# Four buffers for split weight blocks, S5 input by half quarters, and two RG-LRU steps on GpSimd in the first layer

## The chip, the core and the metric

The kernel runs on one core of one Trainium2 chip. The metric is the device time of one execution in microseconds; before the change it is 1570.3 us (median of three runs, 1568.19 to 1570.87).

The core has five engines that run their own instruction queues in order and meet through semaphores. TensorE (PE) multiplies matrices, with its weight loads shown apart (PEld); VectorE (DVE), ScalarE (ACT) and GpSimd (POOL) work element by element; SyncE (SP) issues most of the DMAs, GpSimd the rest. Matrix products leave their sums in PSUM, everything else lives in SBUF, and SBUF holds what DMAs bring from HBM.

## The reference

Two layers over 512 latent and 256 context tokens of width 1024. Each layer norms and modulates its input, projects it with one matrix whose columns feed three branches (attention, RG-LRU, S5), multiplies each branch by its SiLU gate, projects it, merges the three by sigmoid gates, and adds the result back. The two recurrent branches, cut to what the change touches:

```python
def rglru_branch(...):
    u_l = depthwise_conv(x_l, conv_w, conv_b); u_c = depthwise_conv(x_c, conv_w, conv_b)
    for d, rev in enumerate((False, True)):
        a_c, b_c = rglru_coeffs(u_c, ...)        # a = exp(log_a), b = sqrt(1 - a^2) * (i * x)
        h_c = linear_scan(a_c, b_c, None, rev)   # h_t = a_t h_(t-1) + b_t
        h0 = h_c[:, 0] if rev else h_c[:, -1]
        a_l, b_l = rglru_coeffs(u_l, ...)
        hs_l.append(linear_scan(a_l, b_l, h0, rev)); hs_c.append(h_c)
    return hs_l[0] + hs_l[1], hs_c[0] + hs_c[1]

def s5_branch(u_l, u_c, ...):                     # per group of 16 channels, 64 complex states
    for d, rev in enumerate((False, True)):
        ar, ai, bbr, bbi = s5_discretise(...)
        cr_, ci_ = complex_scan(ar, ai, *drive(u_c, bbr, bbi), None, rev)
        lr_, li_ = complex_scan(ar, ai, *drive(u_l, bbr, bbi), (cr_[:, idx], ci_[:, idx]), rev)
        ...
    return readout(u_l, ...), readout(u_c, ...)
```

## The kernel before

Activations are kept transposed, 128 channels to a tile, with the 512 latent and 256 context tokens along the free axis (TT = 768 columns). All large products are made in three passes of float32r matmuls: both operands are split into a high and a low part, and `product` (L170) adds high x high, low x high and high x low, key tile by key tile. A weight block is 128 x 512 numbers (four key tiles of one 128-column output), and an input projection (`inproj`, L771) uses two of them.

`wsplit` (L154) makes a block ready. SyncE loads it into `wr` (L161), ScalarE copies it to the high part `wh` (L162), and the low part `wl` comes from VectorE as `wr - wh` (L167). In layer 0, from after the S5 input projection until `merge_y` of the S5 branch, `by_dma` is set: ScalarE writes `-wh` into `wl` (L164), and GpSimd issues a DMA that adds `wr` to it (L165). The pool `pW` keeps three tiles each of `wr`, `wh` and `wl`; some callers pass another pool or keep their tiles elsewhere.

The RG-LRU (`lru`, L810) runs four times per layer, for 128 channels at a time. It projects, convolves, makes four small products for the gates, and then: `th` gets a square root (L853), `gi` is multiplied by it (L854, 128x1536, both directions at once), two forward scans write `ys` (L855, L856), the reverse scan writes `hb` into `th` (L858), and `ys` and `hb` are added (L859, 128x768). L854 to L859 are VectorE's. Every working tile of this pool has one buffer, so the next RG-LRU waits for this one's.

S5 runs in 16 steps of two groups (`step`, L697). `s5_input` (L592) loads a quarter of the S5 input, 128 channels, into `vt` with eight DMAs from DRAM on SyncE; two buffers of 128x8x128 numbers. `s5_scan(pa)` (L600) multiplies it, turns it (`U`, `Wt`, L623 and L624, from PSUM), scans it (L629), turns it back and leaves the states in `st`; `s5_out(pa)` (L656) makes the outputs and reads `vt` again. The next quarter's input is asked for at the step before its first scan (L705).

RG-LRU calls, S5 steps and the gates' projections are mixed by a table (`PLAN`, L35): in layer 0 all 16 S5 steps lie beside the RG-LRU calls and the products that follow them. On every engine the order of the instructions is fixed when the kernel is built. It isn't the order of the source: a block's `wh` is made several products ahead, as far as the buffers reach.

Of the kernel before, what the change touches and what calls it, by code (L numbers as in the profile page):

```python
# [11 lines left out]
F32 = mybir.dt.float32  # L12
# [17 lines left out]
NCH = 96  # L30
NCC = 32
NCE = 128
# [19 lines left out]
def hybrid_kernel(ctx, tc, xT, cc, wmod, win, winv, wbr, wout, wglu, wlru, par, lqk, s5a, s5b, s5B, s5C, dsk, rope, outT):  # L52
# [101 lines left out]
    def wsplit(src, n, p=None, bufs=3, keep=None):  # L154
        p = p or pW
        raw = p.tile([128, 512], F32, name="wr", tag="wr", bufs=bufs)
        if keep:
            p, bufs = keep, None
        wh = p.tile([128, 512], F32R, name="wh", tag="wh", bufs=bufs)
        wl = p.tile([128, 512], F32R, name="wl", tag="wl", bufs=bufs)  # L160
        SP.dma_start(raw, src)  # L161
        S.activation(wh, raw, AF.Copy)  # L162
        if by_dma[0]:
            S.activation(wl, f32(wh), AF.Copy, scale=-1.0)  # L164
            G.dma_start(wl, raw, accum_op=OP.add)  # L165
        else:
            V.tensor_sub(wl, raw, f32(wh))  # L167
        return wh.rearrange("p (k n) -> p k n", n=n), wl.rearrange("p (k n) -> p k n", n=n)
# [385 lines left out]
    def s5_make(l):  # L554
# [34 lines left out]
                return (sps[pa][:, :R_WS].rearrange("p (q n) -> p q n", q=4),  # L589
                        tps[pa // 2][:, pa % 2 * 2:pa % 2 * 2 + 2])  # L590

        def s5_input(qt):  # L592

            vt = p5.tile([128, 8, NCE], F32, name="vt", tag="vt", bufs=2)
            for s in range(8):
                SP.dma_start(vt[s * 16:(s + 1) * 16],
                             usd[qt * 128:(qt + 1) * 128, s, :].rearrange("(g h) c -> h g c", h=16))
            vts[qt] = vt

        def s5_scan(pa):  # L600
            pr = pa % 4
            vt, (tb, ws) = vts[pa // 4], turn(pa)

            px = mis("ps_x")
            for d in range(2):
                for c in range(2):
                    for g in range(2):
                        v = vt[:, 2 * pr + g, :NCH] if d == 0 else vt[:, 2 * pr + g, NCE - 1:NCE - 1 - NCH:-1]
                        PE.matmul(px[64 * g:64 * g + 64, (c * 2 + d) * NCH:(c * 2 + d + 1) * NCH],  # L609
                                  lhsT=ws[:, 2 * d + g, 64 * c:64 * c + 64], rhs=v, start=True, stop=True)  # L610
            pxv = px[:, :4 * NCH].rearrange("p (c d j) -> p c d j", c=2, d=2)

            sh = [128, 2, 2, NCH]
            Cb = tb[:, 0].unsqueeze(1).to_broadcast(sh)
            Sb = tb[:, 1].unsqueeze(1).to_broadcast(sh)
            U = p5.tile([128, 2, 2, NCH], F32, name="U", tag="U")
            Wt = p5.tile([128, 2, 2, NCH], F32, name="W", tag="W")
            xx = p5.tile([128, 2, 2, NCH], F32, name="xx", tag="xx", bufs=2)
            for d in range(2 if need else 0):
                b = l * 32 + 2 * pa + d  # L620
                S.activation(dec[:, :, d, 1:], ones[:, 0:1].unsqueeze(2).to_broadcast([128, 2, NCH - 1]), AF.Copy,
                             scale=rho[:, b:b + 1])
            V.tensor_mul(U, pxv, Cb)  # L623
            V.tensor_mul(Wt, pxv, Sb)  # L624
            V.tensor_add(xx[:, 0], U[:, 0], Wt[:, 1])
            V.tensor_sub(xx[:, 1], U[:, 1], Wt[:, 0])
            if need:
                xf = xx.rearrange("p c d j -> p (c d j)")
                V.tensor_tensor_scan(xf, dec.rearrange("p c d j -> p (c d j)"), xf, 0.0, op0=OP.mult, op1=OP.add)  # L629
            else:  # L630
                for d in range(2):
                    b = l * 32 + 2 * pa + d
                    for c in range(2):
                        V.tensor_tensor_scan(xx[:, c, d], rho[:, b:b + 1].to_broadcast([128, NCH]), xx[:, c, d], 0.0,
                                             op0=OP.mult, op1=OP.add)
            U2 = p5.tile([128, 2, 2, NCH], F32, name="U2", tag="U")
            W2 = p5.tile([128, 2, 2, NCH], F32, name="W2", tag="W")
            js = slice(0 if need else NCC - 1, NCH - 1)
            V.tensor_mul(U2[..., js], xx[..., js], Cb[..., js])
            V.tensor_mul(W2[..., js], xx[..., js], Sb[..., js])  # L640
            st = sts[pa % 2]
            if not need:
                for g in range(2):
                    ps = slice(64 * g, 64 * g + 64)
                    V.tensor_sub(st[0:64, g, :, js.start + 1:NCH], U2[ps, 0, :, js], W2[ps, 1, :, js])
                    V.tensor_add(st[64:128, g, :, js.start + 1:NCH], U2[ps, 1, :, js], W2[ps, 0, :, js])
                return
            V.tensor_sub(xx[:, 0, :, js], U2[:, 0, :, js], W2[:, 1, :, js])
            V.tensor_add(xx[:, 1, :, js], U2[:, 1, :, js], W2[:, 0, :, js])

            for g in range(2):
                for c in range(2):
                    S.activation(st[64 * c:64 * c + 64, g, :, js.start + 1:NCH], xx[64 * g:64 * g + 64, c, :, js], AF.Copy)
            S.activation(st[:, :, 0, NCH:], st[:, :, 0, :NCC], AF.Copy)

        def s5_out(pa):  # L656

            pr = pa % 4
            vt, (vf, tp), st = vts[pa // 4], reach(pa), sts[pa % 2]
            py = mis("ps_y")  # L660
            for g in range(2):
                o = py[:, g * NCL:(g + 1) * NCL]
                PE.matmul(o, lhsT=tp[:, g, :], rhs=vt[:, 2 * pr + g, NCC:NCC + NCL], start=True,
                          stop=False)
                PE.matmul(o, lhsT=vf[:, g, 32:160], rhs=st[:, g, 0, NCC:NCC + NCL], start=False, stop=False)  # L665
                PE.matmul(o, lhsT=vf[:, 2 + g, 0:128],
                          rhs=st[:, g, 1, NCH - 1::-1] if need else st[:, g, 1, NCH - 1:NCC - 1:-1], start=False,
                          stop=True)
# [28 lines left out]
        def step(pa):  # L697
            if pa == 0:
                s5_input(0)
                s5_scan(0)  # L700
            if l == 0 and done[0] < 16:
                s5_inner(done[0])
                done[0] += 1
            if pa + 1 < 16:
                if pa % 4 == 3:  # L705
                    s5_input(pa // 4 + 1)
                    if l == 0:
                        whole(s5_tables(l, pa // 4 + 1, p5, pr_.tbs))
                s5_scan(pa + 1)
# [8 lines left out]
    for l in range(L):  # L718
# [91 lines left out]
        def lru(i):  # L810
# [40 lines left out]
            V.scalar_tensor_tensor(th, a2, 1.0, th, op0=OP.add, op1=OP.mult)  # L851
            V.scalar_tensor_tensor(gi, gi, 1.0, u.unsqueeze(1).to_broadcast([128, 2, TT]), op0=OP.add, op1=OP.mult)
            S.activation(th, th, AF.Sqrt, scale=0.25, bias=tiny[:, 0:1])  # L853
            V.tensor_mul(gi, gi, th)  # L854
            V.tensor_tensor_scan(ys[:, T:], r[:, 0, T:], gi[:, 0, T:], 0.0, op0=OP.mult, op1=OP.add)  # L855
            V.tensor_tensor_scan(ys[:, :T], r[:, 0, :T], gi[:, 0, :T], ys[:, TT - 1:TT], op0=OP.mult, op1=OP.add)  # L856
            hb = th[:, 0]
            V.tensor_tensor_scan(hb[:, ::-1], r[:, 1, ::-1], gi[:, 1, ::-1], 0.0, op0=OP.mult, op1=OP.add)  # L858
            V.tensor_add(ys[:, :W], ys[:, :W], hb[:, :W])  # L859
            return ys  # L860

        m_t = [pMm.tile([128, W], F32, name="m", tag="m") for _ in range(KT)]
# [482 lines left out]
```

## Time and profile before

| | us |
|---|---|
| median of three runs | 1570.3 (1568.19 to 1570.87) |
| the profiled execution, its own time | 1571.9 |
| its span, first to last instruction | 1570.1 |
| TensorE busy | 1489.2 (95%) |
| VectorE busy | 1125.0 (72%) |
| ScalarE busy | 818.7 (52%) |
| GpSimd busy | 172.2 (11%) |
| mean granted clock of TensorE | 0.98 of full speed |

The busy times say how much work each engine has, not where it waits: TensorE's 81 us of idle time are spread over stages whose limits differ. The profile is read stage by stage, with the windows first and then the waits and the time lines inside one stage.

### The profile page before, as it was taken

How to read it: one execution, taken by the hardware profiler on the slowest of the kernel's cores; microseconds unless marked ns; L12 is line 12 of the kernel's file. 1: busy time of each engine (PE TensorE's matmuls, PEld its weight loads, DVE VectorE, ACT ScalarE, POOL GpSimd, SP SyncE). 2: the span in 40 equal slices, each digit the busy share in tenths (PEclk: the TensorE clock that was granted, in tenths of full speed). 3: DMA queues.
4: the chain of work that ended last, by engine and by line, in shares of the span. 5: the costliest groups of instructions: out<-in, count | busy, mean ns of one | idle time of the engine just before them, and what ended most of it. 6: DMA issues, size and time to landing. Idle time of an engine off the chain costs nothing. (4 is left out here: it accounts for less than half of the span.)

```text
span 1570.1 us, 24750 instructions
## 1 busy us (share of the span) xinstructions
PE 1489.2 (95%) x9096; PEld 1246.2 (79%) x9096; DVE 1125.0 (72%) x2312; ACT 818.7 (52%) x1468; POOL 172.2 (11%) x231
## 2 busy tenths in 40 slices
PE   4998899899999999999999999999999999999997
PEld 2786778788988888888778887777788988888777
DVE  6789899978367757658568863789775488397555
ACT  6676878664344534534325365666525365355433
POOL 1111111124000100000332310000000000000110
PEclk8998999999999999989999999999999999999999
DMA  8555444467311111115573762435454212111542
GB/s 279 167 151 119 112 110 105 89 158 197 94 52 43 42 53 46 49 34 177 193 250 125 258 201 82 143 111 162 118 168 132 81 61 58 65 61 54 174 148 94
DMA packets 111210, 189.13 MB, mean 120 GB/s; under 512 B 25328, under 2 KB 42352, under 8 KB 111088
## 3 DMA queue, kind: packets, MB, share of 16 engines
q1 hardware_dynamic: 97392, 158.17, 32.2%
q0 software_dynamic: 13696, 29.37, 8.1%
q8 instruction: 72, 1.18, 0.3%
q14 instruction: 50, 0.41, 0.1%
HBM read 145.02 MB, written 25.69 MB: 109 GB/s over the span
## 5 line engine op out<-in xcount | busy, mean ns | idle before, releaser
L162 ACT ACTIVATE wh<-wr 128x512 fp32r<-128x512 f32 x320 | 200.3, 629 | 367.2 <-PE ps_in L180 151.3
L180 PE MATMUL ps_in<-hH,wh 128*128 128x512 f32 x1248 | 376.5, 360 | 14.4 <-ACT wh L162 7.3
L180 PE MATMUL ps_in<-hH,wl 128*128 128x512 f32 x1248 | 378.6, 359 | 7.1 <-DMA wl<-wr 7.1
L180 PE MATMUL ps_in<-hL,wh 128*128 128x512 f32 x1248 | 375.5, 359 | 0.0
L167 DVE TENSOR_TENSOR wl<-wr,wh 128x512 fp32r<-128x512 f32 x264 | 187.5, 714 | 172.7 <-ACT wh L162 129.9
L180 PEld LDWEIGHTS ps_in<-hH,wh 128*128 128x128 f32 x1248 | 207.3, 192 | 52.3 <-ACT wh L162 8.4
L180 PEld LDWEIGHTS ps_in<-hH,wl 128*128 128x128 f32 x1248 | 207.7, 191 | 43.1 <-DMA wl<-wr 9.6
L180 PEld LDWEIGHTS ps_in<-hL,wh 128*128 128x128 f32 x1248 | 206.9, 191 | 31.8
L911 POOL TENSOR_TENSOR m<-m,g 128x768 f32<-128x768 f32 (+1 forms) x16 | 29.0, 1811 | 730.7 <-issue 348.4
L1091 ACT ACTIVATE p<-ps_s,mx 128x768 f32<-128x768 f32 (+1 forms) x80 | 65.2, 815 | 71.4 <-DVE mx L1090 67.5
L180 PE MATMUL ps_b<-yH,wh 128*128 128x512 f32 (+1 forms) x288 | 89.5, 359 | 0.6 <-DVE m L945 0.6
L180 PE MATMUL ps_b<-yL,wh 128*128 128x512 f32 (+1 forms) x288 | 88.0, 357 | 0.0
L180 PE MATMUL ps_b<-yH,wl 128*128 128x512 f32 (+1 forms) x288 | 87.7, 357 | 0.0
L1089 DVE TENSOR_REDUCE mx<-ps_s 128x1 f32<-128x768 f32 (+1 forms) x80 | 67.6, 847 | 23.9 <-PE ps_s L1086 23.3
L165 POOL DMA_DIRECT2D wl<-wr x56 | 49.0, 896 | 259.6 <-ACT wl L164 206.1
L180 PEld LDWEIGHTS ps_b<-yH,wh 128*128 128x128 f32 x288 | 48.2, 188 | 10.7 <-ACT wl L164 0.9
L180 PEld LDWEIGHTS ps_b<-yL,wh 128*128 128x128 f32 x288 | 47.7, 188 | 7.2
L180 PEld LDWEIGHTS ps_b<-yH,wl 128*128 128x128 f32 x288 | 47.6, 188 | 7.2
L180 PE MATMUL acc<-mH,wh 128*128 128x512 f32 (+1 forms) x160 | 49.2, 340 | 0.0
L180 PE MATMUL acc<-mH,wl 128*128 128x512 f32 (+1 forms) x160 | 48.8, 337 | 0.0
L180 PE MATMUL acc<-mL,wh 128*128 128x512 f32 (+1 forms) x160 | 48.8, 337 | 0.0
L1107 DVE TENSOR_TENSOR wTL<-ps_t,wTH 128x512 fp32r<-128x512 f32 (+1 forms) x72 | 35.9, 536 | 13.4 <-ACT wTH L1106 13.2
(357 smaller groups left out, 2901.1 us busy)
## 6 DMA issues: line engine op xcount, KB each, us to landing
wr<-in_win SPq DMA_DIRECT2D x208, 256.0 KB
wm<-in_wmod SPq DMA_DIRECT2D x48, 512.0 KB
wl<-wr POOLq DMA_DIRECT2D x56, 256.0 KB, 3.9
wr<-in_wbr SPq DMA_DIRECT2D x48, 256.0 KB
sp<-s5d SPq DMA_DIRECT2D x16, 768.0 KB
wr<-in_wout SPq DMA_DIRECT2D x32, 256.0 KB
s5d<-vv POOLq DMA_DIRECT2D x16, 320.0 KB, 3.2
usd<-up SPq DMA_DIRECT2D x8, 512.0 KB
```

Of the source, the lines that this page charges most:

```text
L162: S.activation(wh, raw, AF.Copy)
L165: G.dma_start(wl, raw, accum_op=OP.add)
L167: V.tensor_sub(wl, raw, f32(wh))
L180: PE.matmul(out[:, c0:c0 + n], lhsT=(wl if ps == 2 else wh)[:, k, :], rhs=rhs(k0 + k, ps == 1)[:, t0:t0 + n], start=st, stop=en)
L911: (V if n == 0 and dt >= ADD_V[l] else G).tensor_add(m_t[dt][:, :W], m_t[dt][:, :W], g[:, :W])
L1089: V.reduce_max(mx[:, 0:1], sc[:, :kw], axis=AX.X)
L1091: S.activation(p[c][:, :kw], sc[:, :kw], AF.Exp, bias=mx[:, 1:2], scale=0.125, accum_out=sm[:, c:c + 1])
L1107: V.tensor_sub(wTL[:, k0:k1, qi * 128:(qi + 1) * 128], src, f32(wTH[:, k0:k1, qi * 128:(qi + 1) * 128]))
```

## The change

`wsplit` gives the high and low parts four buffers where they come from the pool `pW`; the raw tile keeps three. `s5_input` loads half a quarter (64 channels) into a tile of half the size, still with two buffers and eight DMAs each; it is asked for at every even step, for the half quarter that the step after it scans first. In `lru` of layer 0 the product L854 and the sum L859 go to GpSimd (`E = G`); layer 1 keeps them on VectorE. `vt` gives up 4 KB of each partition, and the two added weight tiles take 4 KB.

```diff
--- before.py
+++ after.py
@@ -156,6 +156,8 @@
         raw = p.tile([128, 512], F32, name="wr", tag="wr", bufs=bufs)
         if keep:
             p, bufs = keep, None
+        if p is pW:
+            bufs = 4
         wh = p.tile([128, 512], F32R, name="wh", tag="wh", bufs=bufs)
         wl = p.tile([128, 512], F32R, name="wl", tag="wl", bufs=bufs)
         SP.dma_start(raw, src)
@@ -589,23 +591,24 @@
                 return (sps[pa][:, :R_WS].rearrange("p (q n) -> p q n", q=4),
                         tps[pa // 2][:, pa % 2 * 2:pa % 2 * 2 + 2])
 
-        def s5_input(qt):
-
-            vt = p5.tile([128, 8, NCE], F32, name="vt", tag="vt", bufs=2)
+        def s5_input(hq):
+
+            vt = p5.tile([128, 4, NCE], F32, name="vt", tag="vt", bufs=2)
             for s in range(8):
                 SP.dma_start(vt[s * 16:(s + 1) * 16],
-                             usd[qt * 128:(qt + 1) * 128, s, :].rearrange("(g h) c -> h g c", h=16))
-            vts[qt] = vt
+                             usd[hq * 64:(hq + 1) * 64, s, :].rearrange("(g h) c -> h g c", h=16))
+            vts[hq] = vt
 
         def s5_scan(pa):
             pr = pa % 4
-            vt, (tb, ws) = vts[pa // 4], turn(pa)
+            vt, (tb, ws) = vts[pa // 2], turn(pa)
 
             px = mis("ps_x")
             for d in range(2):
                 for c in range(2):
                     for g in range(2):
-                        v = vt[:, 2 * pr + g, :NCH] if d == 0 else vt[:, 2 * pr + g, NCE - 1:NCE - 1 - NCH:-1]
+                        v = vt[:, 2 * (pr % 2) + g]
+                        v = v[:, :NCH] if d == 0 else v[:, NCE - 1:NCE - 1 - NCH:-1]
                         PE.matmul(px[64 * g:64 * g + 64, (c * 2 + d) * NCH:(c * 2 + d + 1) * NCH],
                                   lhsT=ws[:, 2 * d + g, 64 * c:64 * c + 64], rhs=v, start=True, stop=True)
             pxv = px[:, :4 * NCH].rearrange("p (c d j) -> p c d j", c=2, d=2)
@@ -656,11 +659,11 @@
         def s5_out(pa):
 
             pr = pa % 4
-            vt, (vf, tp), st = vts[pa // 4], reach(pa), sts[pa % 2]
+            vt, (vf, tp), st = vts[pa // 2], reach(pa), sts[pa % 2]
             py = mis("ps_y")
             for g in range(2):
                 o = py[:, g * NCL:(g + 1) * NCL]
-                PE.matmul(o, lhsT=tp[:, g, :], rhs=vt[:, 2 * pr + g, NCC:NCC + NCL], start=True,
+                PE.matmul(o, lhsT=tp[:, g, :], rhs=vt[:, 2 * (pr % 2) + g, NCC:NCC + NCL], start=True,
                           stop=False)
                 PE.matmul(o, lhsT=vf[:, g, 32:160], rhs=st[:, g, 0, NCC:NCC + NCL], start=False, stop=False)
                 PE.matmul(o, lhsT=vf[:, 2 + g, 0:128],
@@ -698,12 +701,13 @@
             if pa == 0:
                 s5_input(0)
                 s5_scan(0)
+            if pa % 2 == 0 and pa < 14:
+                s5_input(pa // 2 + 1)
             if l == 0 and done[0] < 16:
                 s5_inner(done[0])
                 done[0] += 1
             if pa + 1 < 16:
                 if pa % 4 == 3:
-                    s5_input(pa // 4 + 1)
                     if l == 0:
                         whole(s5_tables(l, pa // 4 + 1, p5, pr_.tbs))
                 s5_scan(pa + 1)
@@ -851,12 +855,13 @@
             V.scalar_tensor_tensor(th, a2, 1.0, th, op0=OP.add, op1=OP.mult)
             V.scalar_tensor_tensor(gi, gi, 1.0, u.unsqueeze(1).to_broadcast([128, 2, TT]), op0=OP.add, op1=OP.mult)
             S.activation(th, th, AF.Sqrt, scale=0.25, bias=tiny[:, 0:1])
-            V.tensor_mul(gi, gi, th)
+            E = G if l == 0 else V
+            E.tensor_mul(gi, gi, th)
             V.tensor_tensor_scan(ys[:, T:], r[:, 0, T:], gi[:, 0, T:], 0.0, op0=OP.mult, op1=OP.add)
             V.tensor_tensor_scan(ys[:, :T], r[:, 0, :T], gi[:, 0, :T], ys[:, TT - 1:TT], op0=OP.mult, op1=OP.add)
             hb = th[:, 0]
             V.tensor_tensor_scan(hb[:, ::-1], r[:, 1, ::-1], gi[:, 1, ::-1], 0.0, op0=OP.mult, op1=OP.add)
-            V.tensor_add(ys[:, :W], ys[:, :W], hb[:, :W])
+            E.tensor_add(ys[:, :W], ys[:, :W], hb[:, :W])
             return ys
 
         m_t = [pMm.tile([128, W], F32, name="m", tag="m") for _ in range(KT)]
```

## Rows read from the trace of the kernel before

**Rows 1.** the page's busy table: busy us (share), instructions of each engine

```profile
PE 1489.2 (95%) x9096; PEld 1246.2 (79%) x9096; DVE 1125.0 (72%) x2312; ACT 818.7 (52%) x1468; POOL 172.2 (11%) x231
```

**Rows 2.** windows: stretch, length, busy PE PEld DVE ACT POOL, clock, DMA

```profile
86.00:323.00 237.00, 215.10 (x1536) 178.95 (x1535) 214.43 (x441) 179.43 (x353) 30.68 (x36) 0.96 0.49 111
985.00:1135.00 150.00, 139.94 (x824) 114.03 (x822) 126.89 (x256) 93.81 (x123) 0.00 (x0) 0.97 0.44 132
```

**Rows 3.** waits of TensorE, 86 to 323 us: total, times, longest

```profile
PE ps_in L180 <- ACT wh L162: 7.3, 3, 3.7
PE ps_in L180 <- DMA wl<-wr: 5.2, 4, 2.4
PE ps_y L663 <- DVE W L624: 4.5, 1, 4.5
```

**Rows 4.** time line of TensorE: start us, us, what, count, idle before

```profile
111.51 0.51 PE L180 MATMUL ps_in<-hH,wh 128*128 128x512 f32 x2
111.86 0.51 PE L180 MATMUL ps_in<-hL,wh 128*128 128x512 f32 x2
127.40 0.69 PE L180 MATMUL ps_in<-hH,wh 128*128 128x512 f32 x2 [3.71 <-ACT wh L162]
```

**Rows 5.** time line of ScalarE around the same gap

```profile
126.03 0.80 ACT L621 ACTIVATE dec<-ones,rho 128x190 f32<-128x190 f32 x2 [0.70 <-DVE xx L629]
126.73 1.14 ACT L162 ACTIVATE wh<-wr 128x512 fp32r<-128x512 f32 x2
```

**Rows 6.** time line of VectorE around the same gap

```profile
119.69 1.76 DVE L854 TENSOR_TENSOR gi<-gi,th 128x1536 f32<-128x1536 f32 x1 [0.28 <-ACT th L853]
125.07 0.93 DVE L629 TENSOR_TENSOR_SCAN xx<-dec,xx 128x384 f32<-128x384 f32 x1
```

**Rows 7.** windows of half-clock stretches, first and last of three here

```profile
127.80:138.04 10.24, 6.44 (x20) 4.75 (x19) 9.37 (x27) 6.62 (x18) 2.60 (x3) 0.50 0.78 142
291.64:295.05 3.41, 3.06 (x9) 2.67 (x10) 3.41 (x7) 1.64 (x3) 0.00 (x0) 0.50 0.51 87
```

**Rows 8.** DMA issues: what, count, KB each, median us to landing

```profile
wl<-wr POOLq DMA_DIRECT2D x56, 256.0 KB, 3.9
```

**Rows 9.** waits of SyncE's queue, 86 to 323 us

```profile
SPq L161 <- DMA wl<-wr: 67.0, 21, 6.9
```

**Rows 10.** source line L854, layer 0: ns min/median/max, first and last start

```profile
L854 DVE TENSOR_TENSOR gi<-gi,th x4: 1750/1754/1757, 119.7 to 281.2; 128x1536 f32<-128x1536 f32 x4
```

**Rows 11.** groups of VectorE, 86 to 323 us: busy us, mean ns, idle

```profile
L471 DVE TENSOR_TENSOR vv<-xC,pw 128x640 f32<-128x640 f32 x13 | 10.6, 817 | 0.8 <-PE ps_y L666 0.8
L859 DVE TENSOR_TENSOR ysum<-ysum,th 128x768 f32<-128x768 f32 x4 | 3.8, 946 | 0.0
L623 DVE TENSOR_TENSOR U<-ps_x,tb 128x384 f32<-128x384 f32 x16 | 8.9, 553 | 3.8 <-PE ps_x L609 3.6
L629 DVE TENSOR_TENSOR_SCAN xx<-dec,xx 128x384 f32<-128x384 f32 x16 | 15.2, 951 | 0.2
```

**Rows 12.** source line L911: the merge's addition on GpSimd and on VectorE

```profile
L911 POOL TENSOR_TENSOR m<-m,g x16: 1281/1842/2244, 460.3 to 1515.9; 128x768 f32<-128x768 f32 x10, 128x512 f32<-128x512 f32 x6
L911 DVE TENSOR_TENSOR m<-m,g x6: 939/952/953, 779.7 to 861.0; 128x768 f32<-128x768 f32 x6
```

**Rows 13.** time line of GpSimd at two of its additions

```profile
542.65 2.23 POOL L911 TENSOR_TENSOR m<-m,g 128x768 f32<-128x768 f32 x1 [17.70 <-DVE g L910]
...
748.45 2.24 POOL L911 TENSOR_TENSOR m<-m,g 128x768 f32<-128x768 f32 x1 [2.06 <-DVE mods L137]
```

**Rows 14.** time line of VectorE beside these two additions

```profile
543.09 0.95 DVE L1089 TENSOR_REDUCE mx<-ps_s 128x1 f32<-128x768 f32 x1
...
748.92 2.46 DVE L471 TENSOR_TENSOR vv<-xC,pw 128x640 f32<-128x640 f32 x1
```

**Rows 15.** source line L596: issues of vt on SyncE's queue, both layers

```profile
L596 SPq DMA_DIRECT2D vt<-usd x64: 337/429/1767, 75.4 to 1111.5; - x64
```

**Rows 16.** waits of TensorE in the same stage of layer 1

```profile
PE ps_g L180 <- ACT uHL L830: 2.8, 1, 2.8
```

## The prediction

> **What bounds the kernel now.** The page's busy table comes first: TensorE is busy 95% of the span [rows 1], so the question is where its 81 us of idle time lie and what ends them. Next the table of windows, cut where the stages change. The layer-0 stretch that holds RG-LRU, S5 and the first gates runs from 86 to 323 us; TensorE works 215.1 of its 237 us there, and VectorE is as busy, 214.4 us or 90% [rows 2]. The same stage of layer 1 (985 to 1135) leaves 10 us idle. Third, the waits of TensorE inside the first stretch, which are what this change can reach: 7.3 us in three waits for a high part `wh` (L162), 5.2 us in four waits for a low part `wl` that a DMA accumulates (L165), and one wait of 4.5 us at `ps_y` for S5's product `W` (L624) [rows 3].
>
> Fourth, the place with the largest gap, in the time lines of three engines. A pair of matmuls (512 and 256 columns) takes 0.35 us from start to start, so a layer-0 block of 12 pairs lasts 4.2 us; at 127.40 TensorE had waited 3.71 us for a high part [rows 4]. On ScalarE the two `wh` of 126.73 stand behind `dec` at 126.03, which itself waited for VectorE's scan L629 [rows 5]. VectorE reached that scan at 125.07 because the tail of one RG-LRU lay ahead of it, from the gated product at 119.69 on [rows 6]. So the weight parts come late, but through ScalarE from VectorE. Fifth, the granted clock: it falls to 0.50, the lower level of 1.2 GHz, in three stretches here, each behind or within such a gap; the first and the last are shown [rows 7], the middle one is as long as the last.
>
> **Part 1, four buffers of wh and wl.** A block's parts may now be made when the block four back, not three back, has been used: one block, 4.2 us in layer 0 [rows 4], of additional cover. The chain for a low part is two ScalarE copies (0.63 us each, as [rows 5] gives 1.14 for two), the issue on GpSimd (30.7 us for 36, 0.85 each [rows 2]) and 3.9 us to landing [rows 8]: 6.0 us. With three buffers it starts two blocks, 8.4 us, before its use and has 2.4 us to spare; with four 6.6 us. The longest waits are 3.7 us [rows 3], so each could be covered by one more block. Upper bound: all 12.5 us (7.3 and 5.2 [rows 3]). Lower bound: zero, if the same lateness of VectorE is met at the next operand. I take half, **-6.2 us**, since VectorE, at 90%, is the source of the lateness and a deeper queue only shifts it. The raw tile keeps three buffers. SyncE's weight loads already wait 67.0 us in 21 cases here for an accumulation to land [rows 9]; accumulations that start a block earlier also free raw tiles earlier, so I charge nothing. If that cover were gone, it would be the half that I left out.
>
> **Part 2, GpSimd takes the product and the sum in layer 0.** VectorE loses four products of 1.75 us [rows 10] and four sums, 3.8 us together [rows 11], 10.8 us in all. GpSimd's sum of two 128x768 tiles has a median of 1.84 us where VectorE needs 0.95, and its fastest, at 512 columns, is 1.28 [rows 12]. The slope is 2.2 ns an element, so 128x1536 takes about 3.5 us (estimate). New work on GpSimd: 4 x (3.5 + 1.84) = 21.4 us.
>
> It isn't free for VectorE. At 748.45 GpSimd begins an addition [rows 13], and VectorE's `vv`, which reads two SBUF tiles and takes 0.82 us alone [rows 11], lasts 2.46 us and ends just after it; a reduction of a PSUM tile at 543.09 takes 0.95 us inside another such addition, starting and ending before that ends [rows 14]. So while GpSimd adds, VectorE's instructions with two SBUF tiles stand still and those reading PSUM pass. Of VectorE's 214 us here, `U` (8.9 us [rows 11]), its equal `Wt`, `sz` and small fills, about 23 us, pass; the rest, less the 10.8 that leave, is 180 us or 76% of the stretch. Expected blocking is 0.76 x 21.4 = 16.3 us, so VectorE's balance is 16.3 - 10.8 = +5.5 us. Bounds: -10.8 (GpSimd always meets an idle or a PSUM-reading VectorE) and +10.6 (always blocked). I take +5.5 and put half of it on the path, **+2.7 us**, because VectorE has 22.6 us idle here to absorb some.
>
> No row has a scan beside GpSimd, and S5's scans are 15.2 us of the stretch [rows 11]; I count them as blocked like the other two-tile forms, and were they to pass, the share would be 70% and the balance +4.1. On this the Trainium skill ("SBUF — State Buffer", section "Who interferes with whom") says that any VectorE instruction with two SBUF inputs contends with a GpSimd instruction that reads SBUF, the later one waiting for the whole of the other; that covers scans, and by it the balance is +5.5 and not +4.1. The rows agree with it for products and additions; for scans no run here shows it.
>
> One gain comes with it. The 4.5 us wait at `ps_y` [rows 3] is `U` and `W` standing behind such a tail in VectorE's queue; the product leaves 1.76 us [rows 6] of that tail, and `U` and `W` read PSUM and could run beside GpSimd's product. From 0 to 4.5, I take **-2.2 us**. The RG-LRU chain itself gets longer by 1.8 + 0.9 us, which is covered: the four tails lie some 54 us apart (first and last product in [rows 10]), so the buffers are not wanted at once, and `ysum` is wanted only in `merge_y`.
>
> New waits: on GpSimd's queue the product waits for ScalarE's square root (L853) and the sum for VectorE's reverse scan (L858). Queued behind them are the accumulations of `wl`, which today wait for little but ScalarE's copy. An accumulation caught behind both loses 5.3 us plus what the waits add; four buffers leave 6.6 us. I charge nothing, and price it below.
>
> **Part 3, S5 input by half quarters.** 64 DMAs for `vt` become 128, 0.43 us of SyncE's queue each [rows 15]: 13.7 us more per layer. They carry the same bytes. With two half-size buffers a load must wait for `s5_out` two half quarters back, and weight loads stand behind it on SyncE; it is issued a step before use. Between 0 and +5 us, I take **+0.5 us**, nearer to zero because SyncE's weight loads spend their time waiting for buffers [rows 9], not behind issues.
>
> **Clock and the rest.** In the three half-clock stretches TensorE is busy 12.9 us (6.4 in the first, 3.1 in the last [rows 7], 3.4 between), which at full clock would be half: 6.5 us. They follow the very gaps above; I take **-2 us**. In layer 1 the longest wait is 2.8 us for `uHL` [rows 16], and none is for `wh`, `wl` or `vt`: nothing.
>
> Sum: -6.2 + 2.7 - 2.2 + 0.5 - 2 = -7.2 us. The profiled execution took 1571.9 us in all (span 1570.1), so 1564.7; it lies 1.6 us above the median of the runs, so the forecast is 1563.1 us.
>
> **Rivals.** *VectorE binds and the time stays.* What part 1 covers comes back as waits for VectorE and ScalarE; for it speak 90% and the way the gap at 123 us starts, against it that TensorE names `wh` and `wl` and not VectorE in most of its waits. Part 1 shrinks to -2, the clock to 0, the rest (2.7 - 2.2 + 0.5) nets +1: -1, 1569 us. The same time would come if the three raw tiles kept the fourth pair from being filled, that is, if the change did not do what it says.
>
> *GpSimd's queue becomes the bound.* Accumulations stand behind a product or sum that waits for its input and for VectorE; `wl` lands late, and TensorE waits in the middle of a block. It decides when the hold exceeds the 6.6 us of cover: 5.3 us of execution plus 1.3 us of waiting, which a late square root or scan gives easily. If at each of the four tails half of both operations (5.3 us) reaches TensorE, that is 4 x 2.7 = 10.7; with VectorE's full +5.5, SyncE's +0.5, and -6.2 from the blocks elsewhere, +10.5: 1581 us. For it: VectorE's lateness. Against it: only 36 accumulations in 237 us, one per 6.6 us.
>
> *All waits go.* -12.5 - 4.5 - 6.5 with VectorE's balance at zero: -23.5, 1547 us. VectorE's 90% speaks against it.
>
> **How the numbers follow.** Forecast 0.46, all waits going 0.12, no change 0.21, GpSimd's queue 0.21. Less than 0.2%, about 3 us, can't be told from no change here. So faster 0.58, same 0.21, slower 0.21. The range 1548 to 1578 takes in most of the forecast's spread (part 1 from 0 to -12.5, VectorE's balance from -11 to +11), the unchanged time, and the lower half of the queue rival; the likeliest case alone has 1556 to 1567.
>
> **What the changed profile would show.** Right: waits of TensorE for `wh` and `wl` from 86 to 323 us under 6 us together; GpSimd's product near 3.5 us; VectorE's two-tile instructions stretched beside it; fewer half-clock stretches; the stage 6 to 10 us shorter, and layer 1 as before. Wrong: a stage of the old length with TensorE's waits now on VectorE or on `ws` and `st`; waits for `wl` that grow, with the accumulation's issue behind the product or the sum on GpSimd; or a change of more than 3 us after 400 us, where I expect nothing.

## The result: slower, and where the time went

The changed kernel takes 1592.0 us (median of four runs, 1590.1 to 1595.8) where the one before takes 1570.3: the ratio is 1.0143, 95% interval 1.0119 to 1.0168. The forecast was 1563.1 us with a range that ended at 1578. The sign is wrong, and the time lies outside the range.

The profiled execution has a span of 1590.3 us, 20.2 more than before. The page's busy table, as in [rows 1]:

```profile
PE 1492.1 (94%) x9096; PEld 1250.0 (79%) x9096; DVE 1130.2 (71%) x2304; ACT 816.8 (51%) x1468; POOL 196.0 (12%) x239
```

TensorE works 2.9 us longer on the same matmuls and is idle for 98.2 us in place of 80.9. The first merge of layer 0, where VectorE first reads a gate's result and the stage of [rows 2] ends, starts at 346.6 us and not at 323.2. The table of windows for this stage, and for its two longest half-clock stretches (length, busy PE PEld DVE ACT POOL, clock, DMA):

```profile
86.00:346.50 260.50, 222.02 (x1555) 187.12 (x1554) 221.05 (x437) 182.48 (x362) 53.85 (x44) 0.91 0.45 103
113.60:130.67 17.07, 10.87 (x70) 8.77 (x70) 15.69 (x21) 11.01 (x24) 7.65 (x5) 0.50 0.28 59
243.30:256.95 13.65, 7.79 (x48) 6.55 (x49) 11.88 (x17) 8.11 (x21) 4.61 (x4) 0.50 0.43 95
```

The window is 23.5 us longer than in [rows 2], but it isn't the same work: it holds 19 matmuls more, since TensorE's order is another one. A cut with equal work is the first matmul of the attention's values, `ps_v` (L1019): in every kernel here 2354 matmuls lie ahead of it. The windows up to it, before, in the change, and in e2, which is the change without GpSimd's part:

```profile
0.00:409.80 409.80, 360.80 (x2354) 293.16 (x2355) 340.96 (x844) 278.78 (x509) 69.30 (x93) 0.97 0.58 148
0.00:428.19 428.19, 365.21 (x2354) 299.21 (x2355) 345.98 (x836) 277.97 (x509) 92.43 (x101) 0.94 0.55 142
0.00:399.24 399.24, 360.21 (x2354) 294.32 (x2355) 340.66 (x845) 277.99 (x510) 68.08 (x93) 0.97 0.59 152
```

The change reaches that point 18.4 us later than before: 14.0 us are idle time of TensorE (49.0 to 63.0), 4.4 us are matmuls that last longer. Behind it only 1.8 us are added. The lower level of the clock holds for 44.4 us in four stretches between 86 and 350 us, where it held for 17.1 in three before. TensorE's waits from 86 to 346.5 us, which answer to [rows 3] (total, times, longest):

```profile
PE ps_in L182 <- DMA wl<-wr: 14.4, 8, 6.4
PE ps_x L612 <- ACT ws L533: 11.0, 8, 3.6
PE ps_in L182 <- ACT wh L164: 6.0, 2, 5.1
```

The wait for `wh` is about what it was (7.3), that for `wl` has grown from 5.2 to 14.4, and 11.0 us stand at `ps_x`, which had 2.6 before. The groups of GpSimd in the same window (busy us, mean ns of one, idle before it):

```profile
L167 POOL DMA_DIRECT2D wl<-wr x36 | 31.1, 926 | 145.4 <-ACT wl L166 126.7 <-ACT st L657 14.6 <-ACT yo L673 3.6
L859 POOL TENSOR_TENSOR gi<-gi,th 128x1536 f32<-128x1536 f32 x4 | 15.2, 3792 | 48.9 <-ACT th L857 48.9
L864 POOL TENSOR_TENSOR ysum<-ysum,th 128x768 f32<-128x768 f32 x4 | 7.8, 1949 | 14.1 <-DVE ysum L861 14.1
```

The product takes 3.8 us and the sum 1.95, near the 3.5 and 1.84 of the forecast. What they do to the others is seen in the time line (start us, us, engine, what), here around the first product:

```profile
118.51 3.58 POOL L859 TENSOR_TENSOR gi<-gi,th 128x1536 f32<-128x1536 f32 x1 [18.12 <-ACT th L857]
...
118.46 0.35 DVE L628 TENSOR_TENSOR xx<-U,W 128x192 f32<-128x192 f32 x1
118.73 3.59 DVE L629 TENSOR_TENSOR xx<-U,W 128x192 f32<-128x192 f32 x1
122.42 0.96 DVE L632 TENSOR_TENSOR_SCAN xx<-dec,xx 128x384 f32<-128x384 f32 x1
...
123.41 0.45 ACT L624 ACTIVATE dec<-ones,rho 128x190 f32<-128x190 f32 x1 [1.71 <-DVE xx L632]
123.89 0.60 ACT L533 ACTIVATE ws<-ps_wt 128x512 f32<-128x512 f32 x1
...
124.54 1.55 PE L612 MATMUL ps_x<-vt,ws 128*64 128x96 f32 x16 [2.94 <-ACT ws L533]
```

L628 and L629 are twins. The first takes 0.35 us, the second, caught by GpSimd's product, 3.59. S5's scan L632 stands behind it on VectorE, `dec` waits for the scan on ScalarE, `ws` stands behind `dec`, and TensorE waits 2.94 us for `ws`. In e2, without the stop, the same matmuls wait 1.29 us. The clock isn't lowered by this wait: the half-clock stretch around it began at 113.6 us, before the product. The same chain, with 3.21 us at `dec` and 3.58 at `ps_x`, follows the third product; there the clock falls within the wait, at 243.3. In e2 no wait at `ps_x` in this stage is longer than 1.7 us. The fourth product waits for VectorE first; VectorE then waits for it at the scan, and two accumulations stand behind it:

```profile
289.10 4.61 POOL L859 TENSOR_TENSOR gi<-gi,th 128x1536 f32<-128x1536 f32 x1 [9.07 <-ACT th L857]
293.66 1.76 POOL L167 DMA_DIRECT2D wl<-wr  x2
...
293.75 0.69 DVE L860 TENSOR_TENSOR_SCAN ysum<-r,gi 128x256 f32<-128x256 f32 x1 [3.32 <-POOL gi L859]
...
296.91 1.01 PE L182 MATMUL ps_in<-hH,wl 128*128 128x512 f32 x2 [6.41 <-DMA wl<-wr]
```

So the trace offers three causes: VectorE stands still, the RG-LRU takes longer, and accumulations are held. The experiments were to tell them apart.

### The profile page after: what moved, and what is told of

Read it like the earlier page. It is cut to its first block, busy times and chain, and to the rows that moved or that the text cites. A ratio compares the mean times of both kernels' runs of the same rounds, so it can differ in the third digit from the quotient of the medians.

```text
span 1590.3 us, 24814 instructions
## 1 busy us (share of the span) xinstructions
PE 1492.1 (94%) x9096; PEld 1250.0 (79%) x9096; DVE 1130.2 (71%) x2304; ACT 816.8 (51%) x1468; POOL 196.0 (12%) x239
## 5 line engine op out<-in xcount | busy, mean ns | idle before, releaser
L182 PEld LDWEIGHTS ps_b<-yH,wh 128*128 128x128 f32 x288 | 47.8, 188 | 10.3 <-issue 2.3
L1088 PE MATMUL ps_s<-ks,qs 128*128 128x256 f32 (+1 forms) x144 | 42.5, 367 | 3.3 <-ACT p L1096 1.4
```

Of the source, the lines that this page charges most:

```text
L182: PE.matmul(out[:, c0:c0 + n], lhsT=(wl if ps == 2 else wh)[:, k, :], rhs=rhs(k0 + k, ps == 1)[:, t0:t0 + n], start=st, stop=en)
L1088: PE.matmul(sc[:, c0:c0 + w], lhsT=qs[:, c, qt * 128:(qt + 1) * 128], rhs=kk[:, c, t0:t0 + w], start=True, stop=False)
```

## The experiments

A price below is the difference of two ratios to the kernel before, times 1570.3 us; by the intervals it is good to some 3 to 5 us. The expectations, written earlier, take differences of medians, which are up to 3.2 us less or 2.3 more. "First `ps_v`" is the time of the cut with equal work (409.8 us before), "RG-LRU" the mean time from the end of the square root to the end of the sum over the four calls of layer 0 (7.25 us before), "half clock" the time at the lower level between 86 and 350 us (17.1 before). These three come from one execution of each kernel: e2, e7, e8 and e12, which differ little up to `ps_v`, reach it between 399.2 and 403.6 us.

| run | median us | ratio to before (95%) | price over e2 | first `ps_v` | RG-LRU | half clock |
|---|---|---|---|---|---|---|
| the change | 1592.0 | 1.0143 (1.0119 to 1.0168) | 29.5 | 428.2 | 10.9 | 44.4 |
| e1 | 1600.1 | 1.0190 (1.0169 to 1.0211) |  | 435.4 | 10.7 | 44.4 |
| e2 | 1564.2 | 0.9955 (0.9943 to 0.9967) | 0 | 399.2 | 6.8 | 20.5 |
| e4 | 1578.5 | 1.0048 (1.0031 to 1.0064) |  | 410.7 |  | 10.2 |
| e5 | 1585.7 | 1.0111 (1.0083 to 1.0140) | 24.5 | 423.8 | 9.5 | 41.0 |
| e6 | 1576.0 | 1.0037 (1.0019 to 1.0055) | 12.9 | 411.1 | 8.6 | 27.3 |
| e7 | 1583.1 | 1.0092 (1.0063 to 1.0120) | 21.5 | 403.2 | 6.8 | 20.5 |
| e8 | 1564.5 | 0.9966 (0.9948 to 0.9984) | 1.7 | 401.4 | 7.6 | 20.5 |
| e9 | 1576.3 | 1.0036 (1.0019 to 1.0052) | 12.7 | 412.6 | 10.2 | 30.7 |
| e10 | 1595.6 | 1.0163 (1.0139 to 1.0187) | 32.7 | 435.7 | 13.1 | 47.8 |
| e11 | 1568.2 | 0.9981 (0.9962 to 1.0000) |  | 406.8 |  | 20.5 |
| e12 | 1565.6 | 0.9963 (0.9942 to 0.9983) | 1.3 | 403.6 | 7.6 | 20.5 |
| e13 | 1577.3 | 1.0059 (1.0044 to 1.0074) | 16.3 | 415.0 | 10.2 | 34.1 |
| e14 | 1574.0 | 1.0010 (0.9991 to 1.0029) | 8.6 | 413.2 | 10.1 | 27.3 |
| e15 | 1582.4 | 1.0056 (1.0034 to 1.0078) | 15.9 | 419.4 | 11.3 | 41.0 |

### Which part costs: e1, e2, e4

e1 is the kernel before with GpSimd's part alone, e2 the changed kernel without it, e4 the half quarters alone, that is, the change's lines on `s5_input`, `vt` and `vts` put into the kernel before.

```diff
# e1, in the kernel before          # e2, in the changed kernel
+E = G if l == 0 else V             -E = G if l == 0 else V
                                    +E = V
```

> Before, with only the product and the sum of layer 0's RG-LRU on GpSimd. Theory (GpSimd's two operations stop VectorE and hold the accumulations of wl): 15 to 25 us slower than before, 1585 to 1595 us, and more than with four buffers since the cover is shorter. Rival (SyncE: the 64 more issues of vt and their waits hold the weight loads): within 5 us of before, 1565 to 1575 us.

> After, with product and sum back on VectorE: four buffers and half quarters alone. Theory (GpSimd): all of the loss is gone, 1560 to 1571 us. Rival (SyncE): most of the loss stays, 1582 to 1592 us. Third (each build sets another order of the instructions, and the order is what costs): anything, with the waits of TensorE at other places than in after.

> Before with the S5 input by half quarters alone. Theory: 0 to 3 us slower than before, 1570 to 1574 us. Rival (SyncE): 10 to 20 us slower, 1580 to 1590 us, with waits of SyncE for ps_y ahead of weight loads.

GpSimd's part costs 29.8 us by itself (0.0190 x 1570.3), more than the 15 to 25 expected, and 29.5 on top of the other two; it is the whole loss. Without it the change is faster than both kernels: e2 gains 7.1 us on the kernel before. The half quarters alone lose 7.5 us, between the two expectations, and with them in place the four buffers bring 14.6. Four buffers alone (e3) could not be run: with whole quarters they need 62.25 KB a partition in a place where 58.97 are left. What the halves change is seen among SyncE's waits from 86 to 325 us, before, in e4 and in e2:

```profile
SPq L596 <- PE ps_y L663: 4.7, 1, 4.7
```

```profile
SPq L596 <- PE ps_y L664: 25.0, 6, 7.9
```

```profile
SPq L598 <- PE ps_y L666: 21.5, 6, 6.6
```

The load of `vt` now waits for an earlier `ps_y` six times, with the weight blocks behind it. The rows don't show where the 7.5 us are lost: SyncE's waits for accumulations fall by about as much (67.0 to 47.8 us), and e4 is 0.9 us behind at the first `ps_v` and 6.6 at the end of the span. Fewer bytes in flight or twice as many DMAs: e11 tells which. It is e4 with four half-size buffers, as many bytes as two whole ones.

```diff
-vt = p5.tile([128, 4, NCE], F32, name="vt", tag="vt", bufs=2)
+vt = p5.tile([128, 4, NCE], F32, name="vt", tag="vt", bufs=4)
```

> Half quarters with four buffers for them in place of two (the same bytes in flight as with two whole quarters), three buffers for weight parts, product and sum on VectorE: e4 with the pieces issued further ahead. e4 was 6.7 us over before. If those 6.7 us come from SyncE, which waits for a vt buffer with the weight blocks of the projections queued behind it, four buffers take most of it back: 1569 to 1574. If they come from the doubled count of DMAs and vector operations in the S5 input itself, it stays at 1576 to 1581.

```profile
SPq L596 <- PE ps_y L664: 8.7, 3, 3.8
```

The wait falls from 25.0 to 8.7 us, and 10.5 us of time come back, which is all that the halves had cost (the 3.0 us more are not clear of noise). The issues themselves, 64 DMAs a layer as in e4, cost nothing that shows.

### Product or sum: e5, e6

e5 leaves the product on GpSimd and puts the sum back, e6 the other way round.

```diff
-E.tensor_add(ys[:, :W], ys[:, :W], hb[:, :W])   # e5
+V.tensor_add(ys[:, :W], ys[:, :W], hb[:, :W])
-E.tensor_mul(gi, gi, th)                        # e6
+V.tensor_mul(gi, gi, th)
```

> After, with the product alone on GpSimd in layer 0; the sum is VectorE's again. Without both the kernel took 1564.2 us, with both 1592.0. Theory (the hold of wl's accumulations and the stop of VectorE grow with GpSimd's time, 3.5 of 5.3 us per RG-LRU): two thirds of 28 us, 1580 to 1585 us. Rival (every wait of GpSimd's queue costs alike, whatever its length): half, 1576 to 1580.

> After, with the sum alone on GpSimd. Theory (by time, 1.8 of 5.3 us): a third of 28 us, 1571 to 1575 us. Rival (each wait alike): 1576 to 1580. If the sum is free, since nothing needs it soon: 1562 to 1567.

The product costs 24.5 us, the sum 12.9; together they cost 29.5, less than their sum. The medians lie just above the theory's range for e5 and in its rival's for e6. TensorE's wait for `wl` stays at 6.8 us in e5 and 7.1 in e6 (5.7 in e2); it reaches 14 us and more only where both are GpSimd's, as in e1 (14.5) and the change. In e6 the stop can't be the whole price: the four sums hold VectorE for 4.1 us in all, about the 3.8 that leave it, and the kernel loses 12.9. The RG-LRU takes 8.6 us there, 1.8 more than in e2.

### Held accumulations or the stop: e7, e8

In layer 1 GpSimd does nothing beside the RG-LRU [rows 2], so no accumulation is queued there. e7 moves both operations there, instead of in layer 0.

```diff
-E = G if l == 0 else V
+E = G if l == 1 else V
```

> Product and sum on GpSimd in layer 1 instead of layer 0, with four buffers and half quarters. In layer 1 GpSimd issues no accumulations in this stage (wl is VectorE's), so nothing stands behind the two operations: only the stop of VectorE and the longer chain are left. Theory that held accumulations make most of the loss: 1564 to 1571 us. Rival (the stop of VectorE and its followers make most): 1578 to 1590 us.

It costs 21.5 us, in layer 1, where the way from the first `ps_x` to the first `ps_v` takes 261.4 us (242.7 in e2). So accumulations aren't needed for a loss. But it doesn't isolate the stop, because the next RG-LRU waits for this one's tiles. ScalarE's waits from 985 to 1145 us in e7 have this row, where e2 has 4.8 us for VectorE's sum:

```profile
ACT cv L826 <- POOL ysum L864: 15.7, 3, 6.3
```

e8 holds GpSimd's queue without reading SBUF: two fills of a tile that nothing reads any more, tied to the square root by a copy of one column; product and sum are VectorE's.

```diff
+if l == 0:
+    S.activation(a2[:, 0, 0:1], th[:, 0, 0:1], AF.Copy)
+    G.memset(a2, 0.0)
+    G.memset(a2, 0.0)
```

> Product and sum on VectorE, four buffers, half quarters; in layer 0 GpSimd fills a dead tile (128x1536) twice behind the square root that it would have waited for, so its queue is held about as in after, but it reads no SBUF tile. ScalarE has one added element copy of about 0.2 us per RG-LRU. Theory that held accumulations make most of the loss: 1576 to 1588 us. Rival (the stop of VectorE makes it): 1563 to 1568 us, with VectorE's two-tile instructions at their normal length beside the fills.

```profile
118.31 1.38 POOL L861 MEMSET a<- 128x1536 f32 x1 [18.48 <-ACT a L860]
...
118.12 1.75 DVE L863 TENSOR_TENSOR gi<-gi,th 128x1536 f32<-128x1536 f32 x1
119.79 0.35 DVE L629 TENSOR_TENSOR xx<-U,W 128x192 f32<-128x192 f32 x1
```

GpSimd waits for the square root and works behind it as in the change, though for 3.1 us and not 5.7, and in two of the four calls an accumulation stands between the fills. VectorE's product runs right beside a fill in its usual 1.75 us. The time is e2's within the intervals. A hold of this length costs nothing that can be told, so the theory that held accumulations make most of the loss has e7 and e8 against it. The change's longer hold is not tried by e8.

### The stop without the move: e9, and in pieces: e10

e9 is e8 with a product that reads SBUF in place of the fills, 128x1536 (the expectation doubles that width by mistake). No work leaves VectorE and nothing waits for the added product.

```diff
-    G.memset(a2, 0.0)
-    G.memset(a2, 0.0)
+    G.tensor_mul(a2, a2, a2)
```

> The kernel of e2 (four buffers and half quarters, product and sum on VectorE), to which four products of GpSimd are added in layer 0, one behind each square root: a2 times a2 into a2, 128x3072 like the gated product, of a tile that nothing reads any more. No work leaves VectorE and nothing of the RG-LRU waits for the added product; GpSimd's queue is held just as in e8, but this time by an operation that reads SBUF. Theory that VectorE stands still while GpSimd reads: each added product takes some 3.5 us, a VectorE operation that meets it takes 3 to 4 us in place of 0.3 to 1.8, and since product alone on GpSimd cost 21.5 us over e2 while it took 1.75 us from VectorE each time, the added product costs at least as much: 18 to 30 us over e2, 1582 to 1594. Rival, that the loss comes from the longer chain of the RG-LRU (the product finished 1.75 us later, or the sum): 1562 to 1568, as e2 and e8. Rival, that the stop is there but only its own length counts: 4 x 3.5 = 14 us at most over e2, 1572 to 1578.

```profile
119.07 4.14 POOL L861 TENSOR_TENSOR a<-a 128x1536 f32<-128x1536 f32 x1 [18.53 <-ACT a L860]
...
120.52 2.90 DVE L629 TENSOR_TENSOR xx<-U,W 128x192 f32<-128x192 f32 x1
123.34 0.68 DVE L863 TENSOR_TENSOR_SCAN ysum<-r,gi 128x256 f32<-128x256 f32 x1
```

Where e8's fills cost nothing, these products cost 12.7 us, and L629 lasts 2.90 us in place of 0.35. The other three calls hold VectorE as long (3.10 for 0.55, 3.17 for 0.68, 3.00 for 0.40), 10.2 us in all. So an operation of GpSimd that reads SBUF costs by itself, here 1.2 us for each us that VectorE stands. Not every stop is felt at once: around the one shown TensorE waits 1.29 us for `ws`, as in e2, and its next wait of a us or more ends at 185.7. The price is the second rival's figure, not the 18 to 30 of the theory: the rest of e5's 24.5 is something else.

e10 cuts the product into twelve pieces of 128 columns (the expectation says 24 by mistake) and the sum into six; the cut shows the product, in layer 0.

```diff
-E.tensor_mul(gi, gi, th)
+for d in range(2):
+    for c in range(0, TT, 128):
+        E.tensor_mul(gi[:, d, c:c + 128], gi[:, d, c:c + 128], th[:, d, c:c + 128])
```

> The changed kernel with GpSimd's operations cut up: each gated product of layer 0 as 24 pieces of 128 columns, each sum as some 6. The same elements are read by GpSimd, with many starts more. If what costs is the length of one stop (a VectorE operation that is met by it waits 3 to 4 us and everything behind it too), VectorE gets in between pieces and no operation takes over 0.7 us longer than alone: 1570 to 1582. If what costs is the total time that GpSimd holds the port, nothing is won, and the starts add to it: 1590 to 1605; the stops then spread over more VectorE operations, each some tenths of a us longer.

```profile
L862 POOL TENSOR_TENSOR gi<-gi,th 128x128 f32<-128x128 f32 x48 | 29.3, 643 | 48.8 <-ACT th L857 48.8
L869 POOL TENSOR_TENSOR ysum<-ysum,th 128x128 f32<-128x128 f32 x24 | 15.3, 808 | 4.8 <-DVE th L866 4.8
```

The time lies in the second theory's range. No instruction of VectorE lasts more than 0.3 us longer beside a piece, but GpSimd needs 44.6 us in place of 23.0 and the RG-LRU 13.1, and TensorE waits 16.5 us for `wl`. The loss is no smaller than in whole pieces (32.7 against 29.5, which the intervals don't tell apart). Short operations are no way out.

### The longer RG-LRU: e12 to e15

With the product on GpSimd the scan that follows comes later. e12 and e13 are e8 and e9 with a fill of the scan's tile behind, so that the scan should wait.

```diff
+if l == 0:
+    G.memset(ys, 0.0)
```

> The kernel of e8 with one more fill: behind the two fills of a2, GpSimd fills the tile that the first scan of the RG-LRU writes, so that VectorE's scan has to wait for GpSimd, as it waits for the gated product in the changed kernel. Nothing of GpSimd reads SBUF, VectorE keeps product and sum. What GpSimd does behind the square root then lasts 1.4 + 1.4 + 0.7 = 3.5 us, as its product did, and VectorE's scan comes some 1.7 us later than behind VectorE's own product. Theory that the 8.8 us by which the product alone (e5, 21.5 over e2) exceeds the added read (e9, 12.1 over e2) are the RG-LRU's longer way and VectorE's wait at the scan: 8 to 10 us over e2 and e8, 1571 to 1575. Rival, that a scan later by 1.7 us is absorbed by the other work of VectorE and ScalarE, and that e5's rest lies in which operations the reads happen to meet: 1562 to 1568, as e8.

> The kernel of e9 (an added product of GpSimd that reads SBUF, VectorE keeps its own product) with the fill of the scan's tile behind it: read and wait together, with no work taken from VectorE. If read and wait add up, and make what e5 showed: 9 us over e9, 1583 to 1588, near e5's 1585.7. If the wait is absorbed, 1575 to 1579, as e9, and what e5 lost over e9 is not explained by it.

Both missed. The order on each engine is made anew when a kernel is built, and nothing tied the fill to the square root. The source line of the fill in e12 (ns min/median/max, first and last start):

```profile
L864 POOL MEMSET ysum<- x4: 732/737/737, 15.3 to 30.8; 128x768 f32 x4
```

They are repeats of e8 and e9, then, and say how far the prices of two such kernels differ: 0.4 and 3.6 us. e14 ties five fills to the square root. e15 does so with two multiplications of the halves of `a2` into the scan's tile, that is, reading and waiting together.

```diff
+if l == 0:                                              # e14
+    S.activation(ys[:, 0:1], th[:, 0, 0:1], AF.Copy)
+    for _ in range(5):
+        G.memset(ys, 0.0)
+if l == 0:                                              # e15
+    S.activation(a2[:, 0, 0:1], th[:, 0, 0:1], AF.Copy)
+    for _ in range(2):
+        G.tensor_mul(ys, a2[:, 0], a2[:, 1])
```

> The kernel of e2, in which GpSimd fills the scan's tile five times behind each square root of layer 0 (5 x 0.74 = 3.7 us, an accumulation may stand between), so that VectorE's scan has to wait for GpSimd about as long as it waits for the gated product in the changed kernel (3.5 us behind the square root). This is the wait that e12 missed: the fills of the scan's tile ran there at 15 to 31 us, since nothing tied them to the square root. Here they are tied by a copy of one column of the square root into that tile. GpSimd reads no SBUF. Theory that a later scan (the longer way of the RG-LRU) makes the 9 us by which e5 exceeds e9: 8 to 12 us over e2, 1571 to 1577. Rival, that it is absorbed by other work and only operations that read SBUF cost: 1562 to 1568.

> The kernel of e2, in which GpSimd multiplies the two halves of a2 (read by nothing any more) into the scan's tile, twice 768 columns behind each square root of layer 0: as many elements read as by the gated product, and VectorE's scan waits for them. Read and wait together, with no work taken from VectorE. If the wait adds to the read: 1582 to 1590, near e5. If only the read counts: 1573 to 1580, as e9 and e13.

In e14 the RG-LRU takes 10.1 us and 8.6 us are lost, though VectorE runs at its usual speed beside the fills, its scans too; here at the second call, with TensorE's largest wait for VectorE from 86 to 330 us under it:

```profile
177.60 3.94 POOL L862 MEMSET ysum<- 128x768 f32 x5 [19.56 <-ACT ysum L860]
...
179.85 1.75 DVE L867 TENSOR_TENSOR_SCAN th<-r,gi 128x768 f32<-128x768 f32 x1
181.51 0.67 DVE L520 TENSOR_TENSOR wt<-Bb,pw 128x512 f32<-128x512 f32 x1
```

```profile
PE ps_in L182 <- DVE sz L882: 4.9, 1, 4.9
```

This one wait, 4.9 us, ends at 293.42: `sz` of `merge_y` stands on VectorE behind the late sum and S5's next step. The profiled execution was e14's slowest, 5.8 us above the median, so what share of the 8.6 us the wait makes can't be told.

In e15 the same scan, beside a GpSimd operation that reads, lasts 3.31 us, and VectorE then waits for GpSimd as well:

```profile
237.07 7.33 POOL L862 TENSOR_TENSOR ysum<-a 128x768 f32<-128x768 f32 x2 [4.65 <-ACT a L860]
...
239.44 3.31 DVE L867 TENSOR_TENSOR_SCAN th<-r,gi 128x768 f32<-128x768 f32 x1
244.43 0.69 DVE L864 TENSOR_TENSOR_SCAN ysum<-r,gi 128x256 f32<-128x256 f32 x1 [1.68 <-POOL ysum L862]
```

A later scan alone costs 8.6 us, a read alone 12.7, both together 15.9; e15's median of 1582.4 lies at the lower edge of the range for adding. Whether they add isn't settled: their sum, 21.3, is 5.4 us more, about what the intervals leave open, and the read of e9 already lengthens the RG-LRU (10.2). **What stays open** are the 8.6 us by which e5 (24.5) exceeds e15 (15.9), although e5 has taken four products from VectorE and e15 none. The order of all engines differs between the two, as between any two of these kernels, and with it what a read meets; no run holds the order fixed. How much of e14's price is the wait and how much its order isn't settled for the same reason. With 3.6 us between e9 and e13, differences of that size show nothing.

## Why the prediction was wrong, step by step

**The step that failed** is the forecast's charge for what GpSimd's operations do to the others. It put half of VectorE's balance on the path, +2.7 us, "because VectorE has 22.6 us idle here to absorb some", set -2.2 us against it and charged nothing for the new waits and the longer RG-LRU: +0.5 us in all. e1 and e2 measure +29.8 and +29.5.

- **The size of the stop was right.** Four products hold VectorE for 3.2 to 3.3 us each (3.59 for 0.35 in the first; the last as 3.32 idle at the scan), 13.1 in all, and three of the sums for 1.6 each, 4.9. That is 17.9 us where 16.3 were forecast, and less the 10.8 that leave, +7.1 where +5.5 was.
- **Its weight on the path was not.** An average of idle time doesn't absorb a stop that falls into S5's chain from VectorE over ScalarE to TensorE. Behind the first stop TensorE waits 1.65 us longer than in e2, behind the third 3.58 us in a wait that e2 doesn't have. Where a balance of 7.1 us was measured on VectorE, the change reaches the first `ps_v` 29.0 us later than e2: 24.0 idle, 5.0 of longer matmuls. The stop makes part of that; e9, a stop of 10.2 us without the move, makes 12.7.
- **"The RG-LRU chain itself gets longer by 1.8 + 0.9 us, which is covered"**: it gets longer by 3.7 (10.93 less 7.25), and it isn't covered. e14 has nearly that (10.1) without any stop and loses 8.6 us, with its largest wait for VectorE, 4.9 us, at `merge_y` behind the last call. The 54 us between two tails, on which the prediction leant, don't cover what stands behind a tail in VectorE's queue.
- **The rival "GpSimd's queue becomes the bound"** has the right sign, at 1581 us, but its mechanism is at most a part. The 6.41 us at 296.91 are of its kind, so are 3.25 us at 252.71, for an accumulation issued only when the sum had ended (249.2), and the wait for `wl` grew by 9.2 us; but e7 loses 21.5 us without any accumulation behind, and e8's hold costs nothing. A hold as long as that of product and sum together was not tried alone.
- **The -2.2 us at `ps_y`**: the 4.5 us wait of [rows 3] is gone in the change, and in e2 as well (0.4), where the product is still VectorE's. It wasn't the move that took it away.

**Parts 1 and 3 and the clock.** Their terms, -6.2, +0.5 and -2, make -7.7 us; e2 measures -7.1. That is luck, for the terms by themselves were off: the halves cost 7.5 where +0.5 (bounds 0 to +5) was put, the step that failed being that SyncE's loads "spend their time waiting for buffers [rows 9], not behind issues". The load of `vt` itself now waits for a buffer (25.0 us in e4), and twice as many buffers take the loss back (e11). The four buffers bring 14.6 us with the halves in place, where -6.2 was put. In e2 the waits for `wh` in this stage are gone as forecast (7.3 to 0), those for `wl` are not (5.7, with 5.2 before), and `ws` (5.3, with 2.6 before) and `yo` (2.3) take more. e2 reaches the first `ps_v` 10.6 us earlier than before, 10.0 of them idle time of TensorE (49.0 to 39.0). A part that the prediction didn't look at lies behind the stage: from the first merge to `ps_v` TensorE waits 1.9 to 5.3 us for accumulations in the four kernels with three buffers, and at most 1.1 in the twelve with four. Layer 1 is unchanged, as forecast (149.7 us against 149.2 from its first `ps_x` to its first merge).

**The clock** was to give back 2 us; in the change its lower level holds 27.3 us longer between 86 and 350 us. Each of its four stretches there begins within a gap of TensorE or less than 1 us behind one, as the prediction said of the gaps that it hoped to close; the first two (from 113.6 and 185.3) have their like in e2 (from 112.2 and 183.8), the others (243.3 and 294.5) don't.

On scans the prediction had no row. Now there are: the RG-LRU's scan L867, with two SBUF inputs, takes 3.31 us for 1.73 beside a reading GpSimd (e15) and 1.75 beside a filling one (e14). This agrees with the Trainium skill ("SBUF — State Buffer", section "Who interferes with whom"), which has VectorE's instructions with two SBUF inputs contend with GpSimd's reads, and not with a GpSimd instruction that only writes.

## What to carry to other kernels

Before work is moved to GpSimd, look at what VectorE does at that moment: if it reads two SBUF tiles and something further on waits for it, the stop can count with its full length and more, however idle VectorE is on average; and whatever waits for the slower operation's result is late too. Here 10.8 us off VectorE cost 29.5 us. An added GpSimd operation of about the same length, once reading and once only filling, prices the reading in two runs. Halving a buffer's size without doubling their number halves the bytes in flight; here that cost 7.5 us, which twice as many buffers took back. And when two kernels are cut into stages, cut where both have done the same work: the order on an engine may have moved instructions over the edge.

## What the runs showed of the hardware that was not expected

- A GpSimd fill of 128x1536 (1.38 us) costs a VectorE product that runs beside it nothing (1.75 us, its usual time), while a GpSimd product of the same size holds a 0.35 us addition for 2.90 us (e8 and e9, at the same place).
- The hold works both ways: in the change GpSimd's product lasts 4.61 us where VectorE's instruction had begun first, 3.48 to 3.58 otherwise.
- Many short GpSimd operations are dear: a product as twelve pieces occupies it for 7.3 us (29.3 / 4), as one for 3.8.
